# First product of both MLPs as seven block products in place of eight

## The chip, the core and the metric

The kernel runs on one core of a Trainium2 chip, as one program with one launch. The metric is the time of the whole program on the device in microseconds (us), as the median of several runs. Before the change it is 3434.19 us (three runs, 3428.68 to 3443.48).

The core has five engines that each run their own queue in order: TensorE (PE in the profile, with its weight loads as PEld), VectorE (DVE), ScalarE (ACT), GpSimd (POOL) and SyncE (SP), which here issues DMA transfers. They wait for each other by semaphores. A line number such as L286 is a line of the kernel before.

## What is computed

Two transformer blocks of two layers each, one after the other, on 512 tokens of width 1024, in fp32. The change touches the two MLPs of the second block alone:

```python
def sq_relu_mlp(x, w1, w2):
    return jnp.square(jax.nn.relu(x @ w1)) @ w2
...
x = layer_norm(ALPHA * x + h, ln_mix_g[i], ln_mix_b[i])
x = layer_norm(ALPHA * x + sq_relu_mlp(x, mlp_w1[i], mlp_w2[i]), ln_ffn_g[i], ln_ffn_b[i])
```

`w1` is 1024 x 4096 and `w2` is 4096 x 1024, so the inner width is 32 chunks of 128.

## The kernel before

Activations are held transposed: a chunk is 128 features (partitions) by 512 tokens. fp32 precision comes from three matmuls in a reduced format (fp32r): every operand is split into a rounded part `hi` and a rest `lo`, and a product is `hi*hi + hi*lo + lo*hi` (`mm3`, L317). ScalarE writes `hi` (a copy that rounds), VectorE subtracts it to get `lo` (`split`, L312; `wsplit`, L274 for weights).

`mlp` (L1248) walks the 32 inner chunks in groups of 8, 8, 8, 4, 4. For a group it first makes the first product, `gemm` with `w1` (L339): per inner chunk one weight load from memory (`wload`, L267, 128x8x128, 512 KB, four `wraw` buffers), one split into `whi` and `wlo` (two buffers each), 8 x 3 = 24 matmuls of 512 columns into one PSUM bank `g`, and the epilogue `epi` (L1255): Relu on ScalarE, times the bank on VectorE, which gives the square, and the split into the group's hidden chunk `ah`, `al`. Then the second product, `gemm` with `w2`: 8 output chunks, each over the group's inner chunks, and each added to the residual `x` by VectorE (`resid_alpha`, L1239: L1243 in the first group, L1245 later). In the last group `mlp_norm` (L2098) puts `w2`'s splits into tiles that stay (`keep_weights`, L585: `kwh`, `kwl`), and `token_norm` (L2015) makes the last part of the second product by tokens, with the transposes of `x` (L2034) ahead, and the layer norm behind.

In the first group the first two inner chunks are cut into 384 and 128 tokens (`mm3_cut`, L327), since the last tokens of the norm before arrive late. All eight PSUM banks belong to `g` in these phases. `c2` is a pool of 128x512 tiles, 50 of them here, for hidden chunks, results and kept splits.

The code writes the operations in the order given; a scheduler then moves them in each engine's queue, by when their inputs are there and by their place in the program. What stands in the queues is therefore shown below from the built program.

## Time and profile before

| | us |
|---|---|
| median of three runs | 3434.19 (3428.68 to 3443.48) |
| the profiled execution | 3425.17 |
| its span in the profile | 3423.4 |
| TensorE busy in the span | 3245.2 (95%) |
| VectorE busy | 1996.5 (58%) |
| ScalarE busy | 1273.3 (37%) |
| GpSimd busy | 517.0 (15%) |

MLP 0 runs from 2392 us (first matmuls on the cut chunks) to 2734 (transposes of the last part) and its norm ends some 30 us later; MLP 1 runs from 3046 to the end. The profile's page gives shares over the whole span; windows give them for a stretch; the timeline gives every instruction with its start. Matmul records overlap, so what one costs in a row is read from start to start.

### The profile page before, as it was taken

Reading aid. Unit: us, or ns where it says so; the run is one execution under the profiler, and the core shown is the slowest. Engines: PE = TensorE matmul, PEld = TensorE weight load, DVE = VectorE, ACT = ScalarE, POOL = GpSimd, SP = SyncE. Lnnn points to the kernel's source line nnn. Section 1 sums busy time; section 2 is a strip of 40 time slices with the busy share of each in tenths; the row PEclk is TensorE's granted clock in tenths of the full one; section 3 lists DMA queues with packets and bytes.
Section 4 is the critical chain, followed back from the end, with each engine's and each line's share of the span. In section 5 each row is a group of like instructions: output and inputs, shape, how many; then the busy total and the mean of one; then the engine's idle time right before and its main releaser. Section 6 shows DMA issues by size and latency. Waiting matters only on the chain. (4 is left out here: it accounts for less than half of the span.)

```text
span 3423.4 us, 42939 instructions
## 1 busy us (share of the span) xinstructions
PE 3245.2 (95%) x16689; PEld 2599.0 (76%) x16689; DVE 1996.5 (58%) x3596; ACT 1273.3 (37%) x2249; POOL 517.0 (15%) x647
## 2 busy tenths in 40 slices
PE   8989989999998999999899998999999988999999
PEld 6756668888887777777678876767888766778887
DVE  5478753233338787777864655656344479863335
ACT  4367531211124343333422322464332254642223
POOL 2232100000001443333200001311000022210000
PEclk9999999999999999999999999899999999899999
DMA  5323451222222223332133222212333231023332
GB/s 205 113 69 130 142 160 56 58 72 67 63 74 71 75 75 88 83 89 80 53 93 99 88 79 81 90 38 67 93 94 93 86 92 56 19 68 93 93 98 74
DMA packets 413482, 292.40 MB, mean 85 GB/s; under 512 B 14160, under 2 KB 372496, under 8 KB 413280
## 3 DMA queue, kind: packets, MB, share of 16 engines
q1 hardware_dynamic: 404944, 280.73, 27.4%
q10 hardware_dynamic: 6448, 6.10, 0.6%
q0 software_dynamic: 1888, 2.84, 0.3%
q8 instruction: 131, 2.15, 0.3%
q14 instruction: 71, 0.58, 0.1%
HBM read 285.30 MB, written 4.33 MB: 85 GB/s over the span
## 5 line engine op out<-in xcount | busy, mean ns | idle before, releaser
L285 ACT ACTIVATE whi<-wraw 128x1024 fp32r<-128x1024 f32 (+2 forms) x378 | 393.5, 1041 | 1056.5 <-PE g L324 892.8
L286 DVE TENSOR_TENSOR wlo<-wraw,whi 128x1024 fp32r<-128x1024 f32 (+2 forms) x336 | 406.7, 1211 | 439.1 <-ACT whi L285 435.9
L323 PE MATMUL g<-ah,whi 128*128 128x512 f32 (+1 forms) x1488 | 577.2, 389 | 10.0 <-DVE xT L544 4.4
L325 PE MATMUL g<-ah,wlo 128*128 128x512 f32 (+1 forms) x1488 | 574.7, 387 | 4.0 <-DVE wlo L286 2.2
L324 PE MATMUL g<-al,whi 128*128 128x512 f32 (+1 forms) x1488 | 574.9, 386 | 0.0
L323 PE MATMUL g<-h,whi 128*128 128x512 f32 (+1 forms) x1296 | 456.6, 353 | 2.1 <-DVE cvt L1031 0.8
L325 PE MATMUL g<-h,wlo 128*128 128x512 f32 (+1 forms) x1296 | 454.2, 351 | 3.6 <-DVE wlo L286 3.6
L324 PE MATMUL g<-h,whi 128*128 128x512 f32 (+1 forms) x1296 | 456.7, 353 | 0.9 <-DVE h L527 0.8
L323 PEld LDWEIGHTS g<-ah,whi 128*128 128x128 f32 x1488 | 281.7, 190 | 76.0 <-DVE xT L544 5.4
L325 PEld LDWEIGHTS g<-ah,wlo 128*128 128x128 f32 x1488 | 281.4, 189 | 67.5 <-DVE wlo L286 5.1
L324 PEld LDWEIGHTS g<-al,whi 128*128 128x128 f32 x1488 | 281.7, 189 | 61.6 <-DVE al L315 1.3
L323 PEld LDWEIGHTS g<-h,whi 128*128 128x128 f32 x1296 | 245.3, 189 | 40.8 <-issue 6.0
L325 PEld LDWEIGHTS g<-h,wlo 128*128 128x128 f32 x1296 | 245.3, 189 | 40.2 <-DVE wlo L286 4.3
L324 PEld LDWEIGHTS g<-h,whi 128*128 128x128 f32 x1296 | 245.1, 189 | 39.1 <-DVE h L527 2.9
L286 POOL TENSOR_TENSOR wlo<-wraw,whi 128x1024 fp32r<-128x1024 f32 x48 | 115.2, 2402 | 780.2 <-DVE xT L544 514.3
L323 PE MATMUL g<-act,whi 128*128 128x512 f32 x568 | 224.6, 395 | 2.4 <-ACT qk L1900 2.4
L325 PE MATMUL g<-act,wlo 128*128 128x512 f32 x568 | 224.5, 395 | 1.5 <-POOL wlo L286 1.5
L324 PE MATMUL g<-act,whi 128*128 128x512 f32 x568 | 224.3, 395 | 0.0
L544 DVE SCALAR_TENSOR_TENSOR xT<-g,mod,xT 128x512 f32<-128x512 f32 x184 | 136.7, 748 | 102.9 <-PE g L325 102.3
L323 PEld LDWEIGHTS g<-act,whi 128*128 128x128 f32 x568 | 106.5, 187 | 27.9 <-ACT qk L1900 2.6
L569 DVE TENSOR_TENSOR sil<-g,sil 128x512 f32<-128x512 f32 x66 | 39.8, 602 | 150.7 <-PE g L325 150.7
L325 PEld LDWEIGHTS g<-act,wlo 128*128 128x128 f32 x568 | 106.5, 187 | 27.6 <-POOL wlo L286 1.8
(724 smaller groups left out, 5809.1 us busy)
## 6 DMA issues: line engine op xcount, KB each, us to landing
wraw<-in_mlp_w_dram SPq DMA_DIRECT2D x128, 512.0 KB, 4.0
adaw<-in_ada_w_dram SPq DMA_DIRECT2D x40, 1024.0 KB, 5.2
wraw<-in_ssm_w_in_dram SPq DMA_DIRECT2D x49, 512.0 KB, 4.7
wraw<-in_ffn_w_gate_dram SPq DMA_DIRECT2D x44, 512.0 KB, 3.8
wraw<-in_ffn_w_up_dram SPq DMA_DIRECT2D x44, 512.0 KB, 3.7
R<-cumscr SPq DMA_DIRECT2D x64, 256.0 KB, 4.5
wraw<-in_ffn_w_down_dram SPq DMA_DIRECT2D x28, 512.0 KB, 3.4
adaw<-in_ada_w_dram SPq DMA_DIRECT2D x16, 512.0 KB, 7.9
```

Of the source, the lines that this page charges most:

```text
L285: self.nc.scalar.activation(hv, v, AF.Copy)
L286: (eng or self.nc.vector).tensor_tensor(lv, v, hv.bitcast(F32), op=OP.subtract)
L323: nc.tensor.matmul(ps, hv[i], a.hi[k], start=f, stop=False)
L324: nc.tensor.matmul(ps, hv[i], a.lo[k], start=False, stop=False)
L325: nc.tensor.matmul(ps, lv[i], a.hi[k], start=False, stop=l)
L544: self.nc.vector.scalar_tensor_tensor(x[ai][c], ps, g[ai][:, c:c + 1], x[ai][c], op0=OP.mult, op1=OP.add)
L569: nc.vector.tensor_tensor(t, ps, t, op=OP.mult)
```

## The change

The first four inner chunks are made as before (`whole`, with the cut), and then form a group of their own for the second product. The other 28 go in pairs. For a pair, the product of 1024 input features by 256 inner features by 512 tokens is cut in two along each: four weight blocks of 512 by 128 and four activation blocks of 512 by 256 tokens. Eight block products would give the four result blocks; the change makes seven, of sums and differences of blocks (Strassen's method in Winograd's form). Each is 4 x 3 = 12 matmuls of 256 columns.

`quarters` makes the four differences of activation blocks once per MLP (`yd`, from the fp32 copy of `x`) and splits them (`yq`, 16 `c2` tiles that stay); three blocks are the plain ones. `seven_weights` loads a pair's weights as two tiles of 128x4x256, makes four sums (`ws`) and splits five blocks of 512 (`wsh`, `wsl`) and two plain ones together (`whi`, `wlo`). `seven` runs the products over three PSUM banks per pair, A, B and C, two pairs interleaved; a bank is read between two products that add into it (`p1`, `u2`, `u3`), and VectorE's adds of 256 columns put the four result blocks together in `rl`. The epilogue `epi7` makes Relu and Square on ScalarE, and the split as before. The groups are 4, 6, 6, 6, 6, 4 and the `c2` pool has 34 tiles.

```diff
--- before.py
+++ after.py
@@ -99,9 +99,10 @@
     "direct": 7,
     "z": 3,
     "cut": 2,
-    "mlp_c2": 50,
-    "mlp0": (8, 8, 8, 4, 4),
-    "mlp1": (8, 8, 8, 4, 4),
+    "whole": 4,
+    "mlp_c2": 34,
+    "mlp0": (4, 6, 6, 6, 6, 4),
+    "mlp1": (4, 6, 6, 6, 6, 4),
     "pvst": 1,
 }
@@ -361,6 +362,120 @@
                              True, True)
                     epi(ai, c + j, pt)
             c += cw
+    def quarters(self, act, x4):
+        nc = self.nc
+        n = L // 2
+        part = lambda kb, t: Act(*([h[4 * kb + k][:, t * n:(t + 1) * n] for k in range(4)] for h in (act.hi, act.lo)), n)
+        y = [[[x4[kb][:, 2 * q:2 * q + 2, t * n:(t + 1) * n] for q in range(2)] for t in range(2)] for kb in range(2)]
+        d = [[self.c2(name="yd").rearrange("p (k t) -> p k t", k=2) for _ in range(2)] for _ in range(2)]
+        def make(i, q, a, b, o):
+            nc.vector.tensor_tensor(o, a, b, op=OP.subtract)
+            hi, lo = halves[i][0][q], halves[i][1][q]
+            nc.scalar.activation(hi, o, AF.Copy)
+            nc.vector.tensor_tensor(lo, o, hi.bitcast(F32), op=OP.subtract)
+        T, halves = [], []
+        for i in range(4):
+            h, l = ([self.c2(F32R, "yq").rearrange("p (k t) -> p k t", k=2) for _ in range(2)] for _ in range(2))
+            halves.append((h, l))
+            T.append(Act(*([u[k // 2][:, k % 2, :] for k in range(4)] for u in (h, l)), n))
+        for q in range(2):
+            make(0, q, y[0][1][q], y[0][0][q], d[0][q])
+        for q in range(2):
+            make(1, q, y[1][1][q], d[0][q], d[1][q])
+        for q in range(2):
+            make(2, q, y[1][1][q], y[0][1][q], d[0][q])
+        for q in range(2):
+            make(3, q, y[1][0][q], d[1][q], d[1][q])
+        return {1: part(0, 0), 2: part(1, 0), 3: part(1, 1), 4: T[3], 5: T[0], 6: T[1], 7: T[2]}
+    def seven_weights(self, W, c):
+        nc = self.nc
+        a, b = (self.wload(W[512 * i:512 * i + 512, c:c + 256], 4, 256) for i in range(2))
+        x11, x21, x12, x22 = (v[:, :, P * j:P * j + P] for v in (a, b) for j in range(2))
+        def both(src):
+            h, l = (self.ph.tile([P, 4, P], F32R, tag=f"ws{i}", name=f"ws{i}", bufs=6) for i in "hl")
+            nc.scalar.activation(h, src, AF.Copy)
+            nc.vector.tensor_tensor(l, src, h.bitcast(F32), op=OP.subtract)
+            return h, l
+        def total(x, y, op):
+            s = self.ph.tile([P, 4, P], F32, tag="ws", name="ws", bufs=4)
+            nc.vector.tensor_tensor(s, x, y, op=op)
+            return s
+        w = {1: both(x11)}
+        s1 = total(x21, x22, OP.add)
+        s2 = total(s1, x11, OP.subtract)
+        w[6], w[5] = both(s2), both(s1)
+        wb = self.wsplit(b)
+        w[2], w[4] = ([v[:, :, P * j:P * j + P] for v in wb] for j in range(2))
+        w[7] = both(total(x11, x21, OP.subtract))
+        w[3] = both(total(x12, s2, OP.subtract))
+        return w
+    def seven(self, W, c0, pairs, Y, epi):
+        nc = self.nc
+        n = L // 2
+        half = lambda name: self.ph.tile([P, n], F32, tag="half", name=name, bufs=6)
+        S = {}
+        def product(s, p, bank, first):
+            hv, lv = s["w"][p]
+            a = Y[p]
+            for k in range(4):
+                nc.tensor.matmul(bank, hv[:, k], a.hi[k], start=first and k == 0, stop=False, skip_group_check=True)
+                nc.tensor.matmul(bank, hv[:, k], a.lo[k], start=False, stop=False, skip_group_check=True)
+                nc.tensor.matmul(bank, lv[:, k], a.hi[k], start=False, stop=k == 3, skip_group_check=True)
+        def step(i, p):
+            s = S.setdefault(i, {})
+            add = lambda o, a, b: nc.vector.tensor_tensor(o, a, b, op=OP.add)
+            if p == 1:
+                s["w"] = self.seven_weights(W, c0 + 256 * i)
+                s["A"], s["p1"], s["t"] = self.ps("g")[:, :n], half("p1"), [self.c2(name="rl") for _ in range(2)]
+                product(s, 1, s["A"], True)
+                nc.scalar.activation(s["p1"], s["A"], AF.Copy)
+            elif p == 6:
+                s["B"], s["u2"] = self.ps("g")[:, :n], half("u2")
+                product(s, 6, s["B"], True)
+                add(s["u2"], s["B"], s["p1"])
+            elif p == 5:
+                s["C"] = self.ps("g")[:, :n]
+                product(s, 5, s["C"], True)
+            elif p == 2:
+                product(s, 2, s["A"], False)
+                nc.scalar.activation(s["t"][0][:, :n], s["A"], AF.Copy)
+            elif p == 7:
+                s["u3"] = half("u3")
+                product(s, 7, s["B"], False)
+                add(s["u3"], s["B"], s["p1"])
+                add(s["t"][1][:, n:], s["C"], s["u3"])
+            elif p == 4:
+                product(s, 4, s["B"], False)
+                add(s["t"][1][:, :n], s["B"], s["p1"])
+                epi(2 * i + 1, s["t"][1])
+            else:
+                product(s, 3, s["C"], False)
+                add(s["t"][0][:, n:], s["C"], s["u2"])
+                epi(2 * i, s["t"][0])
+                del S[i]
+        for i in range(pairs + 1):
+            for d, p in ((0, 1), (0, 6), (1, 4), (0, 5), (1, 3), (0, 7), (0, 2)):
+                if 0 <= i - d < pairs:
+                    step(i - d, p)
     def columns(self, name, parts, slot=None, bank=None):
@@ -1251,6 +1366,7 @@
         c0 = 0
         for gn in groups:
             hid = self.new_act(gn, L)
+            whole = 0 if c0 else K["whole"]
             def epi(ai, c, ps):
                 t = self.c2(name="rl")
@@ -1258,7 +1374,15 @@
                 nc.vector.tensor_tensor(t, t, ps, op=OP.mult)
                 self.split(hid.hi[c], hid.lo[c], t)
-            self.gemm(w1, c0 * P, gn, 0, NK, [act], epi, cut=0 if c0 else K["cut"], early=0 if c0 else K["early"])
+            def epi7(c, t):
+                nc.scalar.activation(t, t, AF.Relu)
+                nc.scalar.activation(t, t, AF.Square)
+                self.split(hid.hi[whole + c], hid.lo[whole + c], t)
+            if whole:
+                self.gemm(w1, 0, whole, 0, NK, [act], epi, cut=K["cut"], early=K["early"])
+                Y = self.quarters(act, self.x4)
+            self.seven(w1, (c0 + whole) * P, (gn - whole) // 2, Y, epi7)
             if c0 + gn < 32:
                 self.gemm(w2, 0, NK, c0, gn, [hid], self.resid_alpha(x, c0 == 0))
             else:
```

The order in the queues is the same as before everywhere outside the two MLPs, and the two MLPs have the same order. Three places of MLP 0 (L numbers of the changed rows are those of the changed kernel).

VectorE in the second product of the first group, before: `xT` is the residual, `g` a bank, `wlo` the rest of a split weight of `w2`.

```order
L1243 SCALAR_TENSOR_TENSOR xT_155<-xT_155,g_20535 128x512
L286 TENSOR_TENSOR wlo_20596<-wraw_20593,whi_20595 128x1024
L1243 SCALAR_TENSOR_TENSOR xT_155<-xT_155,g_20567 128x512
L286 TENSOR_TENSOR wlo_20628<-wraw_20625,whi_20627 128x1024
L1243 SCALAR_TENSOR_TENSOR xT_155<-xT_155,g_20599 128x512
L286 TENSOR_TENSOR wlo_20660<-wraw_20657,whi_20659 128x1024
L1243 SCALAR_TENSOR_TENSOR xT_155<-xT_155,g_20631 128x512
L286 TENSOR_TENSOR wlo_20692<-wraw_20689,whi_20691 128x1024
```

The same place now, with `yd`, `yq` of `quarters` and with `wlo_20526`, the last of the group's four `w2` splits:

```order
L382 TENSOR_TENSOR yq_20392<-yd_20378,yq_20390 128x512
L1358 SCALAR_TENSOR_TENSOR xT_155<-xT_155,g_20441 128x512
L382 TENSOR_TENSOR yq_20395<-yd_20379,yq_20393 128x512
L1358 SCALAR_TENSOR_TENSOR xT_155<-xT_155,g_20461 128x512
L1358 SCALAR_TENSOR_TENSOR xT_155<-xT_155,g_20475 128x512
L382 TENSOR_TENSOR yq_20396<-yd_20380,yq_20394 128x512
L1358 SCALAR_TENSOR_TENSOR xT_180<-xT_180,g_20495 128x512
L1358 SCALAR_TENSOR_TENSOR xT_180<-xT_180,g_20509 128x512
L287 TENSOR_TENSOR wlo_20526<-wraw_20523,whi_20525 128x1024
L414 TENSOR_TENSOR ws_20579<-ws_20577,wraw_20569 128x512
```

Before, splits and residual updates take turns. Now the operations of `quarters` stand between them, and the split `wlo_20526` comes behind six of the eight residual updates.

VectorE from the end of a second product into the next first product, before:

```order
L286 TENSOR_TENSOR wlo_21364<-wraw_21361,whi_21363 128x1024
L1245 TENSOR_TENSOR xT_180<-xT_180,g_21319 128x512
L286 TENSOR_TENSOR wlo_21400<-wraw_21397,whi_21399 128x1024
L286 TENSOR_TENSOR wlo_21436<-wraw_21433,whi_21435 128x1024
L1258 TENSOR_TENSOR rl_21392<-rl_21392,g_21367 128x512
L315 TENSOR_TENSOR al_21346<-rl_21392,ah_21345 128x512
L286 TENSOR_TENSOR wlo_21472<-wraw_21469,whi_21471 128x1024
L1258 TENSOR_TENSOR rl_21428<-rl_21428,g_21403 128x512
L315 TENSOR_TENSOR al_21348<-rl_21428,ah_21347 128x512
```

The same border now, at the start of the second group of 6, where `u2`, `u3` and `p1` are the half results of the first pair:

```order
L1360 TENSOR_TENSOR xT_180<-xT_180,g_21186 128x512
L287 TENSOR_TENSOR wlo_21348<-wraw_21329,whi_21347 128x1024
L409 TENSOR_TENSOR wsl_21340<-ws_21337,wsh_21339 128x512
L444 TENSOR_TENSOR u2_21272<-g_21271,p1_21255 128x256
L409 TENSOR_TENSOR wsl_21344<-ws_21335,wsh_21343 128x512
L414 TENSOR_TENSOR ws_21478<-wraw_21470,wraw_21472 128x512
L414 TENSOR_TENSOR ws_21480<-ws_21478,wraw_21470 128x512
L409 TENSOR_TENSOR wsl_21354<-ws_21351,wsh_21353 128x512
L444 TENSOR_TENSOR u3_21299<-g_21271,p1_21255 128x256
L409 TENSOR_TENSOR wsl_21360<-ws_21357,wsh_21359 128x512
L444 TENSOR_TENSOR rl_21257<-g_21286,u3_21299 128x256
```

Before, a weight split stands ahead of each hidden chunk. Now most weights of the first pair stand earlier, beside the second product, and the first pair's adds alternate with the weights of the second and third.

VectorE at the end of a first product, ahead of the second product's first residual update, before:

```order
L1258 TENSOR_TENSOR rl_21572<-rl_21572,g_21547 128x512
L315 TENSOR_TENSOR al_21356<-rl_21572,ah_21355 128x512
L286 TENSOR_TENSOR wlo_21652<-wraw_21649,whi_21651 128x1024
L1258 TENSOR_TENSOR rl_21608<-rl_21608,g_21583 128x512
L315 TENSOR_TENSOR al_21358<-rl_21608,ah_21357 128x512
L286 TENSOR_TENSOR wlo_21684<-wraw_21681,whi_21683 128x1024
L1258 TENSOR_TENSOR rl_21644<-rl_21644,g_21619 128x512
L315 TENSOR_TENSOR al_21360<-rl_21644,ah_21359 128x512
L1245 TENSOR_TENSOR xT_155<-xT_155,g_21655 128x512
```

Now, at the end of a group of 6:

```order
L444 TENSOR_TENSOR rl_21509<-g_21555,u3_21585 128x256
L444 TENSOR_TENSOR rl_21509<-g_21523,p1_21507 128x256
L287 TENSOR_TENSOR wlo_21676<-wraw_21673,whi_21675 128x768
L444 TENSOR_TENSOR rl_21508<-g_21555,u2_21524 128x256
L316 TENSOR_TENSOR al_21217<-rl_21509,ah_21216 128x512
L316 TENSOR_TENSOR al_21215<-rl_21508,ah_21214 128x512
L1360 TENSOR_TENSOR xT_155<-xT_155,g_21653 128x512
```

The multiplication that squares has left VectorE, adds of 256 columns and the split of the second `w2` chunk stand ahead of the last two hidden chunks, and these two come in a row.

## Rows read from the trace of the kernel before

**Rows 1.** Page, busy us, share of the span and instructions of each engine

```profile
PE 3245.2 (95%) x16689; PEld 2599.0 (76%) x16689; DVE 1996.5 (58%) x3596; ACT 1273.3 (37%) x2249; POOL 517.0 (15%) x647
```

**Rows 2.** Windows: a stretch of MLP 0 (column names in the first line)

```profile
core 0: us, PE busy (x) PEld busy (x) DVE busy (x) ACT busy (x) POOL busy (x), PEclk, DMA share, GB/s
2424.00:2468.00 44.00, 44.00 (x190) 35.40 (x189) 18.42 (x21) 13.23 (x17) 0.00 (x0) 1.00 0.33 96
```

**Rows 3.** Waits, 2392 to 2740: who waited for whom; us, times, longest

```profile
PEld y L2037 <- ACT kwh L593: 1.1, 1, 1.1
PEld g L324 <- DVE al L315: 0.2, 1, 0.2
```

**Rows 4.** Timeline, TensorE, MLP 0: start us, us; first and last of 45

```profile
2449.61 0.39 PE L324 MATMUL g<-al,whi 128*128 128x512 f32 x1
...
2459.88 0.39 PE L323 MATMUL g<-ah,whi 128*128 128x512 f32 x1
```

**Rows 5.** Timeline, TensorE, 256 columns: first and last of 24

```profile
527.81 0.28 PE L323 MATMUL g<-h,whi 128*128 128x256 f32 x1
...
530.50 0.28 PE L325 MATMUL g<-h,wlo 128*128 128x256 f32 x1
```

**Rows 6.** Timeline, TensorE, 256 columns: first two and last of 24

```profile
1590.96 0.39 PE L323 MATMUL g<-h,whi 128*128 128x256 f32 x1
1591.19 0.28 PE L324 MATMUL g<-h,whi 128*128 128x256 f32 x1
...
1593.78 0.28 PE L325 MATMUL g<-h,wlo 128*128 128x256 f32 x1
```

**Rows 7.** Groups by line: weight loads; busy us, mean ns | idle before

```profile
L325 PEld LDWEIGHTS g<-h,wlo 128*128 128x128 f32 x1296 | 245.3, 189 | 40.2 <-DVE wlo L286 4.3
```

**Rows 8.** Groups by line and shape: VectorE and ScalarE

```profile
L286 DVE TENSOR_TENSOR wlo<-wraw,whi 128x1024 fp32r<-128x1024 f32 x312 | 385.9, 1237 | 419.5 <-ACT whi L285 416.3 <-ACT xt L1085 1.8
L286 DVE TENSOR_TENSOR wlo<-wraw,whi 128x768 fp32r<-128x768 f32 x8 | 7.6, 953 | 3.9 <-ACT whi L285 3.8
L315 DVE TENSOR_TENSOR al<-rl,ah 128x512 fp32r<-128x512 f32 x64 | 44.3, 693 | 44.7 <-ACT ah L314 44.7
L1258 DVE TENSOR_TENSOR rl<-rl,g 128x512 f32<-128x512 f32 x64 | 43.6, 681 | 11.2 <-ACT rl L1257 11.2
L1243 DVE SCALAR_TENSOR_TENSOR xT<-xT,g 128x512 f32<-128x512 f32 x32 | 21.9, 686 | 62.6 <-PE g L325 62.5
L1139 DVE TENSOR_TENSOR H<-H,hS 128x256 f32<-128x256 f32 x48 | 20.1, 418 | 3.5 <-DVE H L1136 0.5
L285 ACT ACTIVATE whi<-wraw 128x1024 fp32r<-128x1024 f32 x354 | 374.9, 1059 | 976.5 <-PE g L324 831.7 <-issue 108.6 <-PE v L1708 13.7
L285 ACT ACTIVATE whi<-wraw 128x768 fp32r<-128x768 f32 x8 | 6.8, 845 | 19.3 <-issue 10.4 <-PE g L324 8.8
L314 ACT ACTIVATE ah<-rl 128x512 fp32r<-128x512 f32 x64 | 40.4, 632 | 87.3 <-DVE rl L1258 87.3
L1257 ACT ACTIVATE rl<-g 128x512 f32<-128x512 f32 x64 | 37.1, 580 | 11.6 <-PE g L325 11.6
L564 ACT ACTIVATE sil<-g 128x256 f32<-128x256 f32 x22 | 8.1, 366 | 1.5 <-PE g L325 1.5
```

**Rows 9.** Timeline, VectorE, end of MLP 0: three splits in a row

```profile
2737.07 1.89 DVE L594 TENSOR_TENSOR kwl<-wraw,kwh 128x512 fp32r<-128x512 f32 x3
```

**Rows 10.** Timeline, TensorE, behind an idle of 3.12 us

```profile
1084.61 0.79 PE L325 MATMUL g<-h,wlo 128*128 128x512 f32 x1 [3.12 <-DVE wlo L286]
...
1087.76 0.42 PE L323 MATMUL g<-h,whi 128*128 128x512 f32 x1
```

**Rows 11.** Page, DMA issues: KB each, median us to landing

```profile
wraw<-in_mlp_w_dram SPq DMA_DIRECT2D x128, 512.0 KB, 4.0
```

**Rows 12.** Timeline, TensorE, end of MLP 0: transposes, first kept weights

```profile
2734.25 1.91 PE L2034 MATMUL y<-ident,xT 128*128 128x128 f32 x16
2737.00 0.50 PE L2037 MATMUL y<-kwh,ah 128*128 128x512 f32 x1 [0.84 <-ACT kwh L593]
```


## Prediction

> **What bounds the kernel now.** I read the page's busy table first: TensorE is busy for 95% of the span and VectorE for 58% [rows 1]. That is a mean over stages, so the two MLPs were cut out by windows. In the first one TensorE is busy for all 44.00 us of a 44 us window, ScalarE for 13.23 and VectorE for 18.42, at a granted clock of 1.00 [rows 2]; the second MLP reads the same. The list of waits from 2392 to 2740 agrees: behind the first cut chunks TensorE's weight queue waits for a kept split of w2 at the very end, 1.1 us, and for a hidden chunk at one group border, 0.2 us [rows 3]. So in these stages a matmul less is time less, as long as the two engines beside it keep up, and they have more than half of their time free.
>
> What a matmul costs is read from start to start, since the records overlap. In the first MLP 45 matmuls of 512 columns start in 10.27 us, 0.2334 us each [rows 4]. The changed products have 256 columns. The kernel has such runs elsewhere, each matmul with a weight load of its own: 24 of them start in 2.69 us, 0.1170 us each [rows 5]; the least even run that I found takes 2.82 us for 24, 0.1226 each [rows 6].
>
> **The products.** A pair of inner chunks takes 2 x 8 x 3 = 48 matmuls of 512 columns before and 7 x 4 x 3 = 84 of 256 after. That is 48 x 0.2334 = 11.20 us against 84 x 0.1170 = 9.83, a gain of 1.37 us. 28 of the 32 chunks of each MLP go that way, 14 pairs, so 28 pairs in all: 38.5 us. With 0.1226 it is 0.90 a pair, 25.3 us. The second product keeps its matmuls; only its groups change.
>
> The shorter matmul leaves less time to load weights behind. One load takes 0.189 us [rows 7], longer than the pace of 0.117, and yet the run of [rows 5] holds it, so loads lie under running matmuls there. The Trainium skill (TensorE: Matmul & The Clock Gate, "Measured speedup vs the span model") says that a load overlaps running matmuls only where their row groups differ, which speaks against this change, as all loads here fill 128 rows. By that rule the 24 loads alone would take 4.5 us; the trace has 2.69 and disagrees.
>
> **VectorE and ScalarE.** Durations are from [rows 8]. A pair now needs on VectorE five weight splits of 512 (0.693 each), one of 1024 (1.237), four weight sums of 512 (priced as the splits), five adds of 256 out of PSUM (0.418) and two hidden splits: 11 x 0.693 + 1.237 + 5 x 0.418 = 10.95 us. Before it was two of 1024 and two times (0.681 + 0.693): 5.2. ScalarE goes to 5 x 0.632 + 1.059 + 2 x 0.366 + 6 x 0.632 = 8.7 us. So VectorE alone would take longer for a pair (10.95) than TensorE (9.83). What decides is how much of it stands beside the second product. There TensorE runs 8 x 18 x 0.2334 = 33.6 us per group of 6, while VectorE has 8 x (0.953 + 0.686) = 13.1 us of work. The order of the changed program puts all weights of a group's first pair and much of the second's there. From the first u2 to the last hidden split stand 36 VectorE rows: 15 of 256, 18 of 512, three weight splits of 1024, 768 and 768, in all 15 x 0.418 + 18 x 0.693 + 1.237 + 2 x 0.953 = 21.9 us, against 3 x 9.83 = 29.5 us of products. I take no cost for the middle of a group. If this cover went, each pair would wait for VectorE (the rival below).
>
> **Where a wait appears.** (1) The first group. The sixteen operations of quarters, 512 wide, stand on VectorE ahead of the last w2 split of that group (wlo_20526), for which TensorE waits. From the end of the fourth whole chunk the last hidden split is done after 0.58 + 0.68 + 0.63 + 0.69, some 2.9 us with the steps between engines. Then come 17 operations of 512, 6 residual updates and two splits of 1024: 17 x 0.693 + 6 x 0.686 + 2 x 1.237 = 18.4 us; at the pace of the three splits in a row of [rows 9] (0.60 from start to start) 16.8. On the way VectorE waits 0.7 us for ScalarE's first rounding and about 1.2 until a whi buffer is free. That is 21.6 to 23.2 us. TensorE has 76 x 0.2334 + 14 x 0.117 = 19.4 us to run in that time, so it waits 2.2 to 3.8. Behind an idle of 3.12 us the trace shows seven matmuls of 512 whose starts take 3.15 us in place of 7 x 0.2334 = 1.63 [rows 10], the lower of the two clock levels (1.2 in place of 2.4 GHz), 1.5 us more. Bounds 2.2 and 5.3; I take 3.0, near the denser pace, since VectorE has a full queue there. (2) The end of a group of 6. ScalarE has, after product 4 of the last pair, one split of 768 and two chains of Relu, Square and rounding, 0.845 + 6 x 0.632 = 4.6 us; product 3 and the 13 matmuls on the first four chunks cover 1.4 + 3.0. With the last split I take 0.5 us, bounds 0 and 1; 4 times per MLP. (3) The start of a group. u2 stands behind a residual update, a split of 1024 and one of 512 (0.69 + 1.24 + 0.69 + 0.42 = 3.0 us), while TensorE runs products 1, 6 and 5, 4.2 us. That hides it, unless a wraw load (median 4.0 us to land, [rows 11]) comes late; 0.2 us, bounds 0 and 1, 4 times per MLP. (4) The last group. Before, 2.75 us lie between the transposes and the first matmul on kept weights [rows 12]. Now ScalarE has 0.42 + 6 x 0.63 + 0.62 = 4.8 us after product 4, of which product 3 covers 1.4; with the steps some 3.7, so 1.0 more, bounds 0 and 2.
>
> **Moved at no cost.** SP still issues two loads of 512 KB per pair, in the order in which they are used, and eight of 384 KB per group for w2; the load on the wire stays as in [rows 2], under half busy. Two whi buffers serve w2 and half of the pair's weights: a w2 chunk has 4.2 us for 0.845 + 0.953 of splitting. Three banks per pair of the eight are enough for two pairs in flight. 34 c2 tiles hold 16 of quarters, 12 hidden and 6 results; the kept splits of w2 need slots that quarters gives back with the last product 4, before they are due. Eight more residual updates per MLP (0.686, as in the first group) lie on VectorE beside the second product. The order outside the two MLPs is the same row for row.
>
> **The sum.** 38.5 - 2 x (3.0 + 4 x 0.5 + 4 x 0.2 + 1.0) = 38.5 - 13.6 = 24.9 us. The profiled execution took 3425.2 us (its span is 3423.4), so 3400.3; the median of the runs shown, 3434.2, is 9 us above it, and the same difference gives 3409.3. That is my forecast.
>
> **Rivals.** *The gain is eaten by small waits.* The run of [rows 6] opens with a start that is 0.23 behind the one before; if each change of bank costs so much, a matmul averages 0.1226, the gain is 25.3, and with 5.3 us in the first group it is 25.3 - 2 x (5.3 + 2.0 + 0.8 + 1.0) = 7.1: 3427. For it: twelve matmuls per bank in place of 24 or 18. Against: most runs of 24 hold 0.117 throughout. *The VectorE queue sets the pace, slower than before.* If the splits don't get ahead, a pair costs 10.95 us plus three waits of 0.7 for ScalarE's rounding, 13.05, on 18 pairs (those that are not the first of a group): 18 x 3.2 = 58 us, and 38.5 - 13.6 - 58 = -33, 3467. It decides from 24.9 / 18 = 1.4 us per pair, so from a pace of 11.2 us. For it: 10.95 is more than 9.83, and VectorE takes its rows in order. Against: the 21.9 us in 29.5. *The waits are hidden better than I think:* all but the ends vanish, 38.5 - 2 = 36.5: 3398. *Weight loads are not hidden:* 84 x 0.189 = 15.9 us against 11.20, 28 x 4.7 = 131 us, 3565. Nothing but the load's length speaks for it. The rule of the Trainium skill named above (TensorE: Matmul & The Clock Gate) would be this case.
>
> **Chances.** My forecast 0.58, hidden better 0.07, eaten 0.26, VectorE's pace 0.08, loads 0.01. A measurement of this kernel tells some 0.5%, 17 us, from no change: the first two are faster by more (0.65), eaten is within it (0.26), the last two are slower (0.09). The range runs from hidden better, 3398, to the eaten case with a little more lost at the group borders, 3431; about 2 in 10 lie outside.
>
> **What would show it.** In the changed profile the run of a product should start its matmuls 0.117 us apart; 0.123 is the first rival. TensorE's idle on wlo in each MLP's first group should be one stall of 2 to 4 us, with the clock perhaps lower behind it. In the middle of groups TensorE should not wait for u2, u3 or wsl; waits of over a microsecond there, pair after pair, are VectorE's pace. Behind product 3 some 0.5 us should be seen on ah or al, and about 3.7 us ahead of the kept weights. An MLP from its first matmul to its last transposes should take some 12 us less. The forecast is wrong if these waits sum to over 20 us, or if a stage outside the MLPs moves.

## The result, and the profile after

The changed kernel takes 3410.8 us (median of 5, 3403.9 to 3413.2) against 3434.2 before; the ratio is 0.9938, 95% interval 0.9924 to 0.9952. A second measurement of the same kernel, below, gives 0.9943 (0.9928 to 0.9958). The forecast was 3409.3. The profiled execution took 3412.7 us, its span 3410.9. One of the twelve executions of e_pool, an experiment below, took 15220 us and stands in no time or ratio given here.

The page answers [rows 1] and [rows 11]: engine, busy us, share, instructions; then the weight loads of both MLPs, now in two sizes, with the median us to landing.

```profile
PE 3225.0 (95%) x17697; PEld 2637.3 (77%) x17697; DVE 2164.5 (63%) x3968; ACT 1391.9 (41%) x2505; POOL 515.7 (15%) x647
...
wraw<-in_mlp_w_dram SPq DMA_DIRECT2D x80, 512.0 KB, 3.8
...
wraw<-in_mlp_w_dram SPq DMA_DIRECT2D x64, 384.0 KB, 3.5
```

TensorE has 1008 matmuls more and 20 us less of busy time; VectorE has 168 us more. Where these lie is seen in the windows of one full group of MLP 0, which answer [rows 2]: the whole group, the stretch of its 21 block products (three pairs), that of its second product, and, from another answer, ten microseconds at the head of MLP 0.

```profile
core 0: us, PE busy (x) PEld busy (x) DVE busy (x) ACT busy (x) POOL busy (x), PEclk, DMA share, GB/s
2518.69:2582.34 63.65, 63.57 (x398) 56.88 (x396) 42.98 (x68) 31.16 (x51) 0.00 (x0) 1.00 0.35 100
2518.69:2548.53 29.84, 29.84 (x254) 29.83 (x252) 21.44 (x38) 18.66 (x32) 0.00 (x0) 1.00 0.29 81
2548.53:2582.34 33.81, 33.73 (x147) 27.05 (x145) 21.54 (x31) 12.50 (x20) 0.00 (x0) 1.00 0.40 116
...
2410.00:2415.00 5.00, 5.00 (x26) 5.00 (x25) 2.52 (x3) 2.17 (x3) 0.00 (x0) 0.50 0.16 54
2415.00:2420.00 5.00, 5.00 (x14) 4.03 (x14) 2.52 (x3) 2.17 (x3) 0.00 (x0) 0.50 0.37 116
```

TensorE is busy throughout a group, and VectorE has 21.44 us of work in the 29.84 us of products (the prediction had 21.9 in 29.5). The last two rows belong to the clock and come up below. The waits of TensorE in MLP 0 from 2420 on, which answer [rows 3], are three:

```profile
PE y L2161 <- ACT kwh L708: 1.7, 1, 1.7
PE g L326 <- DVE wlo L287: 1.2, 1, 1.2
PE g L438 <- ACT p L449: 0.5, 1, 0.5
```

The timeline of TensorE shows where they stand (start, duration, and in brackets the idle time and its releaser). MLP 0 first, down to its end, then the same stall in MLP 1.

```profile
2450.28 0.50 PE L326 MATMUL g<-ah,wlo 128*128 128x512 f32 x1 [1.20 <-DVE wlo L287]
...
2450.83 0.62 PE L325 MATMUL g<-al,whi 128*128 128x512 f32 x1
2451.25 0.63 PE L326 MATMUL g<-ah,wlo 128*128 128x512 f32 x1
...
2456.57 0.28 PE L438 MATMUL g<-yq,wsh 128*128 128x256 f32 x1
...
2518.69 0.28 PE L438 MATMUL g<-act,wsh 128*128 128x256 f32 x1
...
2548.53 0.39 PE L324 MATMUL g<-ah,whi 128*128 128x512 f32 x1
...
2551.32 0.98 PE L324 MATMUL g<-ah,whi 128*128 128x512 f32 x2
2552.14 0.39 PE L325 MATMUL g<-al,whi 128*128 128x512 f32 x1
...
2729.53 1.91 PE L2158 MATMUL y<-ident,xT 128*128 128x128 f32 x16
2733.15 0.50 PE L2161 MATMUL y<-kwh,ah 128*128 128x512 f32 x1 [1.71 <-ACT kwh L708]
...
3096.03 0.38 PE L438 MATMUL g<-act,whi 128*128 128x256 f32 x1 [0.47 <-ACT p L449]
...
3097.74 0.50 PE L326 MATMUL g<-ah,wlo 128*128 128x512 f32 x1 [1.20 <-DVE wlo L287]
...
3102.49 0.28 PE L438 MATMUL g<-yq,wsh 128*128 128x256 f32 x1
```

From 2518.69 to 2548.53 stand 252 matmuls of 256 columns, 0.1184 us from start to start, between the 0.1170 of [rows 5] and the 0.1226 of [rows 6]. Each MLP stalls once, in its first group, 0.47 + 1.20 = 1.67 us. Behind it the 20 matmuls of 512 up to the next product take 6.29 us in MLP 0 (2450.28 to 2456.57), starts 0.42 apart from 2450.83 on, and 4.75 in MLP 1 (3097.74 to 3102.49).

**Lengths.** From the first cut matmul of an MLP to its first closing transpose, read off each kernel's timeline; "products" is the sum from start to start over the matmuls of 256 columns in MLP 1 (1176 of them, 1344 in e_eight4, 1260 in e_whole2), with TensorE's idle in it. The kernels below the third row are experiments, under the labels that they have below. Two are left out: in e_eight the first closing transposes come 92 matmuls sooner in the order, so its lengths don't compare, and e_dve12 has windows of its own.

| kernel | ratio to before, 95% | MLP 0 | MLP 1 | products, MLP 1 |
|---|---|---|---|---|
| before | 1 | 342.16 | 342.35 | |
| changed | 0.9938 (0.9924 to 0.9952) | 334.12 | 327.94 | 141.48, idle 1.67 |
| again (changed) | 0.9943 (0.9928 to 0.9958) | 334.18 | 328.02 | 141.50, idle 1.68 |
| e_groups | 1.0001 (0.9990 to 1.0013) | 346.56 | 341.90 | |
| e_eight4 | 1.0005 (0.9995 to 1.0015) | 349.12 | 343.87 | 159.50, idle 0 |
| e_second | 0.9964 (0.9951 to 0.9977) | 346.57 | 328.02 | 141.48, idle 1.68 |
| e_noq | 0.9914 (0.9902 to 0.9927) | 330.01 | 324.79 | 138.63, idle 0 |
| e_early | 0.9949 (0.9935 to 0.9962) | 335.26 | 332.62 | 139.24, idle 0 |
| e_pool | 0.9966 (0.9956 to 0.9975) | 337.75 | 333.66 | 140.93, idle 1.37 |
| e_split | 0.9931 (0.9919 to 0.9943) | 330.76 | 325.97 | 139.29, idle 0 |
| e_whole2 | 0.9959 (0.9947 to 0.9972) | 334.47 | 334.76 | 160.81, idle 6.67 |
| e_dve6 | 0.9994 (0.9984 to 1.0005) | 338.24 | 343.67 | 148.32, idle 4.43 |

MLP 1 of e_groups, its first cut matmul and its closing transposes:

```profile
3053.32 0.99 PE L336 MATMUL g<-act,whi 128*128 128x384 f32 x2
...
3395.22 2.67 PE L2034 MATMUL y<-ident,xT 128*128 128x128 f32 x23
```

and the same of the changed kernel:

```profile
3047.51 0.99 PE L337 MATMUL g<-act,whi 128*128 128x384 f32 x2
...
3375.45 3.33 PE L2158 MATMUL y<-ident,xT 128*128 128x128 f32 x29
```

Against before, the profiled MLP 0 is 8.0 us shorter and MLP 1 14.4. The difference between the two is the subject of the first experiments.

### The profile page after: what moved, and what is told of

It reads as the page before. It is cut to its first block, busy times and chain, and to the rows that moved or that the text cites. A ratio compares the mean times of both kernels' runs of the same rounds, so it can differ in the third digit from the quotient of the medians.

```text
span 3410.9 us, 45764 instructions
## 1 busy us (share of the span) xinstructions
PE 3225.0 (95%) x17697; PEld 2637.3 (77%) x17697; DVE 2164.5 (63%) x3968; ACT 1391.9 (41%) x2505; POOL 515.7 (15%) x647
## 5 line engine op out<-in xcount | busy, mean ns | idle before, releaser
L286 ACT ACTIVATE whi<-wraw 128x1024 fp32r<-128x1024 f32 (+2 forms) x366 | 367.0, 1003 | 884.5 <-PE g L325 668.7
L287 DVE TENSOR_TENSOR wlo<-wraw,whi 128x1024 fp32r<-128x1024 f32 (+2 forms) x324 | 374.8, 1157 | 300.0 <-ACT whi L286 296.2
L1360 DVE TENSOR_TENSOR xT<-xT,g 128x512 f32<-128x512 f32 x80 | 54.8, 685 | 83.5 <-PE g L326 83.5
L316 DVE TENSOR_TENSOR pl<-pT,ph 128x512 fp32r<-128x512 f32 x128 | 87.2, 686 | 13.2 <-ACT ph L315 11.3
L438 PE MATMUL g<-yq,wsh 128*128 128x256 f32 x336 | 95.0, 283 | 0.0
L439 PE MATMUL g<-yq,wsh 128*128 128x256 f32 x336 | 94.9, 282 | 0.0
L440 PE MATMUL g<-yq,wsl 128*128 128x256 f32 x336 | 94.8, 282 | 0.0
```

The costliest lines, as they stand in the source:

```text
L286: self.nc.scalar.activation(hv, v, AF.Copy)
L287: (eng or self.nc.vector).tensor_tensor(lv, v, hv.bitcast(F32), op=OP.subtract)
L316: self.nc.vector.tensor_tensor(lo, src, hi.bitcast(F32), op=OP.subtract)
L438: nc.tensor.matmul(bank, hv[:, k], a.hi[k], start=first and k == 0, stop=False, skip_group_check=True)
L439: nc.tensor.matmul(bank, hv[:, k], a.lo[k], start=False, stop=False, skip_group_check=True)
L440: nc.tensor.matmul(bank, lv[:, k], a.hi[k], start=False, stop=k == 3, skip_group_check=True)
```

## Experiments: grouping, clock, and the seventh product

**Regrouping alone (e_groups).** Before, with the new groups:

```
-    "mlp0": (8, 8, 8, 4, 4),
-    "mlp1": (8, 8, 8, 4, 4),
+    "mlp0": (4, 6, 6, 6, 6, 4),
+    "mlp1": (4, 6, 6, 6, 6, 4),
```

> Both MLPs in groups of 4, 6, 6, 6, 6, 4 inner chunks, with eight whole products of 512 columns as before. Theory A (the gain is in the products, regrouping is nearly free): the MLPs keep their length within 1.5 us each, 3434 to 3437 us, and no idle of TensorE at the group borders over 0.3 us. Rival B (regrouping costs, or gives, several us per MLP, and so hides or feigns part of what the products give): over 3440 or under 3428.

Measured: 3433.8 us, ratio 1.0001. Theory A, as far as the time goes. But MLP 0 took 346.56 us and MLP 1 341.90, although no product was changed. The windows of this kernel, at the head of MLP 0, show why (columns as above):

```profile
2405.00:2410.00 5.00, 5.00 (x26) 5.00 (x26) 2.52 (x3) 2.17 (x3) 0.00 (x0) 0.52 0.18 54
2410.00:2415.00 5.00, 5.00 (x14) 4.03 (x15) 2.52 (x3) 2.17 (x3) 0.00 (x0) 0.50 0.31 106
```

The kernel before, in the same place of its own profiled execution:

```profile
2410.00:2415.00 5.00, 5.00 (x23) 4.04 (x22) 3.21 (x4) 2.61 (x4) 0.00 (x0) 1.00 0.52 136
```

For some 10 us TensorE ran at half its clock (the lower level, 1.2 GHz), and the changed kernel shows the same stretch at 2410. So the profiled execution of before was the lucky one, and 346.56 is the MLP 0 to compare with: 334.12 is 12.4 us less, and MLP 1's 327.94 is 14.0 less than 341.90.

**The changed kernel once more (again)**, to see whether the change brings that clock.

> The changed kernel once more, beside the kernel before on the same chip. Theory A (the first MLP of the profiled execution ran 10 us at a granted clock of 0.50 for reasons that have nothing to do with the change, since the kernels with whole products show the same stretch): ratio 0.993 to 0.995; the first MLP takes 334 us when that stretch is there and about 330 when it isn't, the second 328. Theory B (the change brings the low clock): the stretch is there again and the ratio is nearer to 0.996.

Measured: 3412.6 us, 0.9943. The low stretch is there again (MLP 0 334.18), so this run does not show the 330 us without it; that the change isn't its cause rests on e_groups, e_second and e_eight4, whose MLP 0 has no seven products and the same stretch.

**Seven products in one MLP (e_second).** The first MLP keeps its whole products, in the new groups; the second is as changed.

> Seven block products in the second MLP alone; the first keeps eight whole products, in the new groups. Theory A (each MLP gives half): 3434 less 12 to 15, 3419 to 3422 us; first MLP from its first matmul to its transposes 342 us, second 328. Rival B (the first MLP gives only 8, the second 14, whatever the clock): 3419 to 3420 and in the changed kernel the first MLP is again near 334 in other runs. Rival C (the gain of one MLP is lost later in the program): 3428 or more.

Measured: 3420.1 us, 12.4 less than before at 0.9964 (7.9 to 16.8), theory A; MLP 1 is 328.02 again. C falls: nothing is given back later. The time alone would fit B too. What speaks against B is the first MLP's 346.57: that is the low clock again, so its "8 and 14" was a comparison with a lucky execution.

**Eight block products of 256 columns (e_eight).** Same blocks, all eight, sums left to PSUM: no weight sums, no quarters.

```
-                Y = self.quarters(act, self.x4)
-            self.seven(w1, (c0 + whole) * P, (gn - whole) // 2, Y, epi7)
+            self.eight(w1, (c0 + whole) * P, (gn - whole) // 2, act, lambda ai, c, ps: epi(ai, whole + c, ps))
```

> The same groups as the changed kernel, the 14 pairs of each MLP by eight block products of 256 columns in place of seven: 96 matmuls per pair, no sums, differences or adds. Theory A (the gain is the missing product): 96 x 0.1184 = 11.37 us a pair against 11.20 of 48 matmuls of 512 columns, 28 x 0.17 = 4.7 us more than the kernel with these groups and whole products, so 3437 to 3442 us; seven products are then worth 28 x 12 x 0.1184 = 39.8 us less their stalls of about 5. Rival B (the gain is the shorter matmul): faster than with whole products, under 3430.

Measured: 3450.6 us, ratio 1.0056 (1.0043 to 1.0069), 9 us above theory A's range. The timeline of TensorE shows a wait that I had not counted, eight times per MLP, 3.8 us in all:

```profile
2457.55 0.28 PE L499 MATMUL g<-act,whi 128*128 128x256 f32 x1
2458.30 0.39 PE L500 MATMUL g<-act,wlo 128*128 128x256 f32 x1 [0.48 <-DVE wlo L287]
```

Both halves of a pair's weights now go through the two shared whi and wlo buffers. With these waits the products take 164.2 us per MLP, where theory A has 1344 x 0.1184 = 159.1: 10 us in both MLPs. So the experiment had a flaw of its own; the next one (e_eight4) gives the pair's splits four buffers:

```
-            sp = [self.wsplit(v) for v in raw]
+            sp = []
+            for v in raw:
+                hi, lo = (self.ph.tile([P, 4, 256], F32R, tag=f"e{i}", name=f"e{i}", bufs=4) for i in "hl")
...
+                sp.append((hi, lo))
```

> Eight block products of 256 columns per pair again, with four pairs of buffers of their own for the split weights. In the run with two shared buffers TensorE stood 0.48 us behind a weight split twice per group, and the matmuls of the products came to 158 to 164 us per MLP in place of 157. Theory A (the 16 us that eight blocks cost beyond the count are those waits): they go, the products run 0.118 us apart, 28 x (96 x 0.1184 - 48 x 0.2331) = 5 us over the kernel of before, 3435 to 3442 us. Rival B (256 columns are dearer per column by themselves, and seven products win in spite of it): the idle is gone and the time stays at 3446 or more.

Measured: 3433.6 us, ratio 1.0005. The idle is gone and 1344 matmuls start 0.1187 us apart, 159.5 us per MLP, against 672 x 0.2333 = 156.8 for the whole products of e_groups. The 288 matmuls of one group, from the first to the next product:

```profile
2514.34 0.28 PE L503 MATMUL g<-act,eh 128*128 128x256 f32 x1
...
2548.51 0.39 PE L324 MATMUL g<-ah,whi 128*128 128x512 f32 x1
```

So the shorter matmul gains nothing by itself. It costs 2.7 us per MLP in the products, and the MLPs are 2.6 and 2.0 us longer than in e_groups, 0.13% of the time, which the interval of 0.9995 to 1.0015 allows; the 1.4 us under theory A's range lie inside that interval too. What the change gains is the missing product: 168 matmuls per MLP, 159.5 - 139.3 = 20.2 us (139.3 is e_split's, which has no stall), of which the width takes 2.7.

## Experiments: the stall of the first group

**Without quarters (e_noq).** Products 4 to 7 read plain quarters of the activations.

```
-                Y = self.quarters(act, self.x4)
...
+                Y = {1: part(0, 0), 2: part(1, 0), 3: part(1, 1), 4: part(0, 1), 5: part(0, 1), 6: part(0, 0), 7: part(1, 1)}
```

> The changed kernel without the quarters: products 4, 5, 6 and 7 take plain quarters of the activations in place of their differences, so this part of the computation is left out and the output differs. Theory A (the whole stall of the first group comes from the sixteen VectorE operations): no gap of TensorE there, no low clock behind, 1.7 to 3.3 us less per MLP, 3403 to 3408 us. Rival B (the last w2 split is late for another reason, a buffer or a load): the gap of 1.20 us stays, 3409 to 3412.

Measured: 3402.3 us, 0.9914, 0.7 us under theory A's range. Both gaps are gone, and so is the low clock behind them; MLP 0 is 4.2 us shorter than in the second run of the changed kernel, MLP 1 3.2. Theory A: the stall is the quarters' doing. Not all of the 3.2 to 4.2 us is stall: without quarters the matmuls of every full group start 0.1179 us apart in place of 0.1184, some 0.6 us per MLP, and why was not tried.

**Quarters earlier (e_early)**, between the two cut chunks and the two whole ones, where VectorE has idle time:

```
-                self.gemm(w1, 0, whole, 0, NK, [act], epi, cut=K["cut"], early=K["early"])
+                self.gemm(w1, 0, K["cut"], 0, NK, [act], epi, cut=K["cut"], early=K["early"])
                 Y = self.quarters(act, self.x4)
+                self.gemm(w1, K["cut"] * P, whole - K["cut"], 0, NK, [act], lambda ai, c, ps: epi(ai, K["cut"] + c, ps))
```

> As the changed kernel, with the sixteen VectorE operations of the quarters issued behind the two cut chunks and ahead of the two whole ones, so that they are not in front of the last weight split of the first group. Theory A (the stall of 0.47 + 1.20 us in each MLP's first group is VectorE's queue, filled by the quarters): no idle at the first group's second product, and 2 to 3.5 us less than the changed kernel, some 3407 to 3409 us. Rival B (the queue stalls the whole chunks instead, whose weight splits now stand behind): the same wait appears at the third chunk, 1 to 4 us per MLP, 3411 to 3418.

Measured: 3415.0 us, rival B's time and its mechanism, in another place than it said. TensorE, MLP 1:

```profile
3079.91 0.39 PE L326 MATMUL g<-ah,wlo 128*128 128x512 f32 x1
3084.20 1.22 PE L324 MATMUL g<-ah,whi 128*128 128x512 f32 x2 [3.90 <-ACT ah L315]
```

The stall of 1.67 has gone from the product, and 3.90 us have come where TensorE wants the last hidden chunks: their multiplication and split on VectorE stand behind most of the quarters.

**The first w2 splits on GpSimd (e_pool):**

```
-                self.gemm(w2, 0, NK, c0, gn, [hid], self.resid_alpha(x, c0 == 0))
+                self.gemm(w2, 0, NK, c0, gn, [hid], self.resid_alpha(x, c0 == 0), eng=None if c0 else self.nc.gpsimd)
```

> As the changed kernel, with the low halves of the w2 weights of each MLP's first group made on GpSimd, which stands idle there, in place of VectorE. Theory A (the stall of 0.47 + 1.20 us is VectorE's queue in front of the last of these splits): both gaps go, no new one appears, an MLP is 1.7 us shorter, 3 us in all, 3406 to 3409 us. Rival B (a split takes about 2.4 us on GpSimd, twice VectorE's, and TensorE waits for each of the four): 1 to 2 us more per MLP, 3412 to 3415.

Measured: 3419.9 us, 0.9966, worse than either theory. TensorE, MLP 1:

```profile
3085.53 0.50 PE L324 MATMUL g<-ah,whi 128*128 128x512 f32 x1 [1.73 <-ACT ah L315]
...
3087.95 0.79 PE L325 MATMUL g<-al,whi 128*128 128x512 f32 x1 [1.46 <-DVE al L316]
...
3115.80 0.36 PE L438 MATMUL g<-yq,wsh 128*128 128x256 f32 x1 [1.37 <-DVE u L444]
```

TensorE waits for hidden chunks and for u2, not for the splits on GpSimd. The timeline of VectorE at the first two gaps shows what is late:

```profile
3083.52 0.69 DVE L409 TENSOR_TENSOR wsl<-wraw,wsh 128x512 fp32r<-128x512 f32 x1 [3.95 <-ACT wsh L408]
3084.13 0.68 DVE L1374 TENSOR_TENSOR rl<-rl,g 128x512 f32<-128x512 f32 x1
3085.51 2.39 DVE L316 TENSOR_TENSOR al<-rl,ah 128x512 fp32r<-128x512 f32 x1 [0.69 <-ACT ah L315]
```

and the timelines of ScalarE and GpSimd have beside it:

```profile
3082.86 0.63 ACT L408 ACTIVATE wsh<-wraw 128x512 fp32r<-128x512 f32 x1 [4.45 <-DMA wraw<-in_mlp_w_dram]
...
3085.00 2.35 POOL L287 TENSOR_TENSOR wlo<-wraw,whi 128x1024 fp32r<-128x1024 f32 x1 [5.97 <-ACT whi L286]
```

A weight split of the next pair, whose weights come late (ScalarE waits 4.45 us for the load), now stands ahead of the hidden chunk's product rl on VectorE, which waits 3.95 us for it: with the splits moved, the order is another. And al takes 2.39 us in place of 0.69, until 0.55 us after the split on GpSimd has ended at 3087.35. The Trainium skill (SBUF — State Buffer, "SBUF: two separate sides") says that a VectorE operation with two inputs in SBUF and a GpSimd operation that reads SBUF lock each other out for a whole instruction; these rows agree. It is so at all eight moved splits of the two MLPs: the last VectorE operation with both inputs in SBUF that starts during a split ends 0.55 us behind it, 1.13 to 2.89 us long, while rl, which reads a bank, keeps its 0.69. So part of the work moved to GpSimd came back to VectorE as waiting.

**Quarters in two steps (e_split):** the eight subtractions ahead of the second product, the eight low halves in its middle.

```
...
-                Y = self.quarters(act, self.x4)
+                Y, later = self.quarters(act, self.x4)
+                add = self.resid_alpha(x, True)
+                self.gemm(w2, 0, 4, c0, gn, [hid], add)
+                later()
+                self.gemm(w2, 4 * P, 4, c0, gn, [hid], lambda ai, c, ps: add(ai, 4 + c, ps))
...
```

The lines left out at the top put the roundings and low halves into `later` and give every difference tiles of its own.

> The changed kernel with the quarters in two steps: the eight subtractions ahead of the first group's second product, their eight low halves in its middle, between its fourth and fifth output chunk. Theory A (the stall is the length of the queue ahead of the last w2 split, now eight operations shorter, 4.8 us): the gaps of 0.47 and 1.20 go and none over 0.5 us appears, 3404 to 3409 us. Rival B (the queue is as long, something else is now last: the third w2 split, or a quarter for product 6): a gap of 1 to 3 us in another place, 3410 to 3416.

Measured: 3407.6 us, 0.9931. Theory A. In TensorE's timeline of MLP 1 the second product and the next pair's first one now run through, with no idle:

```profile
3090.61 0.28 PE L444 MATMUL g<-act,wsl 128*128 128x256 f32 x1
3090.73 0.39 PE L326 MATMUL g<-ah,wlo 128*128 128x512 f32 x1
...
3100.06 0.28 PE L442 MATMUL g<-act,wsh 128*128 128x256 f32 x1
```

MLP 0 is 3.4 us shorter than in the second run of the changed kernel, MLP 1 2.1. It is the shortest of the complete kernels; the intervals of the two ratios (0.9919 to 0.9943, 0.9928 to 0.9958) overlap, so its lead over the changed kernel rests on the traces.

**One pair more (e_whole2):** `"whole": 2` in place of 4.

> The changed kernel with two whole inner chunks in place of four at the head of each MLP, so 15 pairs by seven products. Theory A (each pair is worth 1.2 us, and product 1, which needs no quarter, fills part of TensorE's wait for the last tokens): 3 to 6 us less, 3404 to 3408. Rival B (the quarters are due 11 us sooner, and VectorE takes some 16 us for them and the weights of the pair): TensorE waits 4 to 10 us per MLP for quarters or hidden chunks, 3417 to 3430.

Measured: 3417.7 us, rival B. TensorE, MLP 1:

```profile
3063.20 0.58 PE L438 MATMUL g<-act,whi 128*128 128x256 f32 x1 [1.87 <-ACT p L449]
...
3070.92 0.58 PE L438 MATMUL g<-yq,wsh 128*128 128x256 f32 x1 [4.80 <-ACT yq L381]
```

A pair worth 1.2 us pays 6.67 us of waiting, 4.80 of it for a quarter and 1.87 for ScalarE's copy p1. Two whole chunks don't cover the quarters; four do, but for the stall of 1.67 us.

## Experiments: how near VectorE is

Six (e_dve6), and twelve (e_dve12), operations of 512 columns more per pair: the last weight difference is made again and again.

```
-        w[3] = both(total(x12, s2, OP.subtract))
+        s3 = total(x12, s2, OP.subtract)
+        for _ in range(6):
+            nc.vector.tensor_tensor(s3, x12, s2, op=OP.subtract)
+        w[3] = both(s3)
```

> As the changed kernel, with six more VectorE operations of 512 columns per pair: the last weight difference is made seven times over. They start 0.60 us apart, so a full group of three pairs gets 10.8 us on top of some 46 of its 63.5 us. Theory A (VectorE's work averages out over a group, because weights are prepared beside the second product): it still fits, at most 6 us more than the changed kernel, under 3418. Rival B (VectorE works pair by pair, the rival of the prediction: 10.95 + 3.6 us a pair plus waits against 9.95): at least 3 us a pair on 18 pairs or more, 3465 or above.

> Twelve more such operations per pair, 21.6 us a group of three pairs, so about 68 of 63.5 us. Theory A (averaged over a group, VectorE binds only when a whole group's work is longer than TensorE's): now it binds, about 4 us a group of 6 and a few us at the first and last ones, 35 to 60 us more than the changed kernel. Rival B (pair by pair): 18 pairs x 8 us or more, 3550 or above. Rival C (VectorE is not needed in time at all, the rows only look late): no change.

Measured: 3429.4 us with six (19 more than the changed kernel) and 3553.2 with twelve (142 more). Windows of a full group with six (the group, the main run of its products):

```profile
2525.28:2589.88 64.60, 64.46 (x397) 56.96 (x396) 52.43 (x86) 30.57 (x51) 0.00 (x0) 1.00 0.34 98
2525.28:2552.69 27.41, 27.41 (x229) 27.23 (x228) 27.28 (x49) 16.56 (x30) 0.00 (x0) 1.00 0.22 63
```

and with twelve (the group, 240 of the 252 matmuls of its products, most of its second product):

```profile
2540.56:2618.10 77.54, 67.46 (x397) 59.08 (x396) 64.22 (x104) 31.31 (x50) 0.00 (x0) 0.93 0.28 82
2540.56:2581.07 40.51, 31.86 (x242) 31.02 (x241) 39.48 (x68) 17.70 (x31) 0.00 (x0) 0.87 0.18 53
2586.96:2618.10 31.14, 29.72 (x127) 23.24 (x126) 20.23 (x29) 10.23 (x14) 0.00 (x0) 1.00 0.41 117
```

With six, VectorE is busy for 27.28 of 27.41 us in the main run of the products (228 of 252 matmuls; the other 24 now stand behind nine of the second product), and TensorE still runs at 0.1202 per matmul; a group is 0.95 us longer, and the first group of 6 pays some 6 us. With twelve, VectorE fills the products (39.48 of 40.51) and sets their length, while it stands idle for a third of the second product (20.23 of 31.14). So theory A is wrong where it averages over a group, and B where it gives VectorE no lead, though twelve land on its figure. What comes near both is the room that the window of the changed kernel shows, 29.84 - 21.44 = 8.4 us in the products, 2.8 a pair: six operations use 3.6, 3 x 0.8 = 2.4 us too much, where the group grew by 0.95, and twelve 7.2, 3 x (7.2 - 2.8) = 13.2 us too much, where the group grew by 77.54 - 63.65 = 13.9. The second match is in part luck: TensorE's idle in that group sums to 10.0 us, and the other 3.9 stand beside a granted clock of 0.87 in the products. Why VectorE doesn't run further ahead beside the second product was not tried. The added rows also shift the program's order a little, which the two runs can't separate.

## Why the prediction was right, point by point

- **The products:** right in kind, optimistic in size. Predicted 14 x 1.37 = 19.2 us per MLP with a pace of 0.1170; 1176 matmuls took 139.8 us without the idle (0.1184 apart in full groups, more behind the stall; 139.3 in e_split, without a stall), against 672 x 0.2333 = 156.8, so it is 17.0. The term was 2.2 us too large per MLP. The pace of a run of 24 in another stage was taken for runs of 252; a part of the difference comes with the quarters as operands (0.1179 in e_noq, without them), and where the rest comes from stays open.
- **Weight loads** lie hidden, as said. The groups by line of the changed kernel have a load of 190 ns for each matmul of the 0.118 pace:

```profile
L440 PEld LDWEIGHTS g<-yq,wsl 128*128 128x128 f32 x336 | 63.9, 190 | 0.0
```

  The Trainium skill's rule that a load overlaps only where row groups differ (TensorE: Matmul & The Clock Gate, "The mechanism", the section ahead of the one that the prediction names) does not describe these runs. The same section also lets a load that targets a background weight buffer go ahead of running matmuls; that would agree with them, but no run here shows the buffer.
- **(1) The first group:** 3.0 predicted per MLP. Measured in MLP 0: 1.67 of idle and 6.29 - 20 x 0.2333 = 1.6 of low clock, 3.3; in MLP 1: 1.67 and 0.1, since the clock stayed at 1.00 there. The place and the cause (e_noq) were right, the lower clock behind it for MLP 0 alone; the idle was 0.5 us under its bounds. Not foreseen was the first piece, 0.47 us: product 2 writes on into the bank of product 1 and waits for ScalarE's copy p1, which elsewhere products 6 and 5 cover.
- **(2) Group ends:** 0.5 each predicted. At 2551.32 two matmuls take 0.82 us in place of 0.47; a group's 144 matmuls of 512 take 33.80 us, against 33.46 in e_eight4, so 0.34 each, 1.4 per MLP in place of 2.0. The shape is the predicted one: ScalarE rounds the last hidden chunk there, until 2551.74.
- **(3) Group starts:** 0.2 predicted, none measured; product runs open at pace.
- **(4) The last group:** 1.0 predicted; transposes to kept weights take 3.62 us (2729.53 to 2733.15) against 2.75 in [rows 12], 0.87 more.
- **The sum:** 2 x 17.0 - 3.3 - 1.8 - 2 x 1.4 - 2 x 0.87 = 24.4 us, where 24.9 was predicted: the products were put too high by 4.4 us, the waits by 4.0. The mechanism was right, but that the sum is met so closely is luck, as two errors cancel. The MLPs against e_groups say the same: 12.4 + 14.0 - 2 x 0.87 = 24.7.
- **What stays open:** the ratios give 21 us (16 to 26) and 20 (14 to 25), some 4 under this sum. The prediction named a stage outside the MLPs that moves as a sign of being wrong, and in the profiled executions they do move, though their order of rows is unchanged. Against e_groups, whose span is 18.9 us longer, the changed kernel starts MLP 0 4.8 us later (2395.41 against 2390.58), which is about what is missing. The ten executions with seven products start it at 2392.95 to 2400.75, the four without at 2389.94 to 2392.09. The stretch between the MLPs took 312.2 us in before, 318.0 in the changed kernel, 316.2 in e_groups and 312.4 in e_second. With one profile per kernel, whether the change lengthens the stages ahead of MLP 0, or the executions differ by chance, is not shown.
- **The rivals:** the first (0.1226 a matmul) is dead; VectorE's pace is real but 2.8 us a pair away; e_split is "hidden better" made true in part.

## What to carry to other kernels

A product saved by sums pays as long as the engine that makes the sums has room in the very stretch where the products run: read its busy time in that window, not over the whole span or group. Where the sums must be made once at the start, cut that work so that what the bounding engine waits for next does not stand behind all of it. And compare a stage with the same stage of a control that only shares the schedule, since one execution can hold a clock drop that the other has not.

## What the runs showed of the hardware

- The head of MLP 0, where TensorE has gaps of 0.25 to 0.9 us while it waits for the last tokens, was followed by some 10 us at a granted clock of 0.50 in 12 of 14 profiled executions, but not in those of before and e_dve6, which have the same gaps; it costs some 4.5 us (MLP 0 took 346.56 in e_groups, 342.16 in before). In e_dve6 such a stretch stands behind the head of MLP 1, in its 343.67.
- A stall does not always lower the clock: the same 0.47 + 1.20 us was followed by 0.50 in MLP 0 and by 1.00 in MLP 1, in both profiles of the changed kernel.
- A VectorE operation with both inputs in SBUF that started during a weight split on GpSimd took 2.39 us in place of 0.69, and ended 0.55 us behind it (e_pool; the other seven splits show the same).
- Two matmuls of 256 columns, each with its own weights, cost 1.5 to 1.7% more than one of 512 (2 x 0.1184 in the changed kernel and 2 x 0.1187 in e_eight4 against 0.2333).
